# Order of the first loads, the sixth product's second accumulator, and the bank of a values' step in a hybrid encoder layer on one core

## The chip, the core and the metric

The kernel runs on one core of a Trainium2 chip. The metric is the device time of one execution in microseconds. All arithmetic that reaches the output is fp32; a product is formed from operands split in a high and a low part ("hi" and "lo"), with three matmuls (hi x hi, hi x lo, lo x hi) that add up in one accumulator in PSUM.

## What is computed

One encoder layer, for a prompt of 512 tokens and a sample of 1024 tokens, width 1024, with shared weights (cut to what matters):

```python
def _trunk(x, ...):
    h = _rmsnorm(x, norm_attn_g)
    z = h @ w_in
    q, k, v, ca, cb = parts of z
    a_out = _window_attn(q, k, v, bias, band, attn_sink)
    c = _dwconv(ca * sigmoid(cb), conv_dw_w, conv_dw_b)
    c = silu(_layernorm(c, conv_ln_g, conv_ln_b))
    x = x + concatenate([a_out, c]) @ w_out
    h = _rmsnorm(x, norm_ffn_g)
    u = _dwconv(h @ w_up, ffn_dw_w, ffn_dw_b)
    x = x + (silu(u[..., :D_FF]) * u[..., D_FF:]) @ w_down
    return _rmsnorm(x, norm_final_g)
```

## The kernel before

The work is laid out with channels on the 128 partitions and 512 tokens in a row: column tile `nt` = 0 is the prompt, 1 and 2 are the halves of the sample. Each engine runs its own list of instructions in order; the lists are set ahead of the run by a scheduler. From L1340 on TensorE's list follows the program as it is written, and from L1681 on SyncE's too. So a change of a buffer can move rows on an engine, in places where the source is the same. SyncE (SP) issues nearly all transfers; ScalarE (ACT) issues a few.

**The head.** x of the prompt comes transposed in eight pieces of 128 rows (`load_xT(0)`, L200), the weights of the first two projections in five pieces (`load_first`, L221; `PIECES` gives the first row block and the count of each). `first_pieces` scales and splits them: ScalarE makes the hi part of x (L471) and of the weights (L482), GpSimd the lo part of the weights (L483). `beside` (L516) then runs the two projections side by side over the eight row blocks, three matmuls each and block. It does so first for `nt` = 0, then for `nt` = 1, whose x (`load_xT(1)`, tile names `q<-in_laid_xsT`) comes behind the prompt's rows (`load_rows(0)`).

**The projections.** `step(i, nt)` takes a bank of PSUM, runs the 24 matmuls of one projection (`proj`, L305 to L307), and `evac` takes the result out, by its kind: queries, keys, values, or the convolution's two inputs. From about the middle of this phase, `use["step"]` is `"b"`: projections have the two banks b0 and b1 to themselves, while attention (`attention`, L640, L682, L696, and others) runs on the banks a and u between them. A bank is given back when the last Python reference to its tile goes, and the next request takes the first one that is free.

The values' kind ("v") is one of the last branches of `evac`: VectorE multiplies the projection by the row scales (L443) from PSUM into SBUF, a second bank `pt` is taken, four transposes write it (L446), and ScalarE and VectorE read it for the hi and the lo part (L453, L454). `step` holds the projection's bank until `evac` returns.

**The down-projection.** It is done as seven products of half-size matrices (`ORDER` is 1, 2, 5, 6, 7, 4, 3, so the product with `i` = 4 is the sixth). `down_step` runs step `p` of product `i`; there are 11 steps for a product (one step covers 2 x 128 of the 2816 rows, halved by the method). Here TensorE and SyncE follow the written program; the other lists are scheduled. In a step, `mm_down` adds three matmuls (L1514 to L1516) to each of six blocks `tt` of the output. The accumulators are wide tiles of two banks: `pd[0]` holds `tt` 0 and 1, `pd[1]` holds 2 and 3, `pd[2]` holds 4 and 5. There are four wide tiles in all. A product takes `pd[0]` and `pd[1]` at step 0, and `pd[2]` at step `hold` (3 for `i` = 4), where it makes up for the steps that it left out. When a product ends, `evacuate` reads its three accumulators out, by VectorE's adds at L1059 for `i` = 7, and they are free after that. So the sixth product begins with the one free tile for `pd[0]`, and `pd[1]` is the first one that the fifth product (`i` = 7) gives back. `load_x1` fetches a quarter of the residual in six transfers (L1526), and `with_x` adds it to a finished part in three adds, one on VectorE and two on GpSimd.

The lines that set what is edited:

```python
        if p == 0:
            pd.extend(wide() for _ in range(2))
        hold = 5 if i == ORDER[0] else HZ if i == 4 else HOLD
        if p == hold:
            pd.append(wide())
        for tt in range(4):
            mm_down(pd[tt // 2][:, (tt % 2) * NT:(tt % 2 + 1) * NT], i, p, tt)
```

Of the kernel before, what the change touches and what calls it, by code (L numbers as in the profile page):

```python
# [18 lines left out]
NT = 512  # L19
# [40 lines left out]
SA, N2, SA2 = 4, 99, 4  # L60
KL, WN = 16, 7
LN = 3
SUM_AT = (4, 6, 8, 10, 12, 14, 16, 18)
XP, HZ = (1, 3, 3, 6), 3
LZ = 6
# [39 lines left out]
def tile_hybrid_encoder(ctx: ExitStack, tc: tile.TileContext, xs, rel_bias, norm_attn_g, w_in,  # L105
# [19 lines left out]
    def bank(job):  # L125
        return banks.tile([NT], among=use[job])
# [91 lines left out]
    def load_first(i, queue):  # L218
        k0, n = PIECES[i]
        first_w.append(sb.tile([n, 2 * P]))  # L220
        queue.dma_start(first_w[i][:], laid["w_first"][k0:k0 + n].rearrange("k p c -> p k c"))  # L221

    nc.scalar.activation(warm[:], nhalf[:], AF.Exp)
    x_of_prompt = load_xT(0)
    for i in range(2):
        next(x_of_prompt)
        load_first(i, nc.sync)
    for i in range(2, len(PIECES)):
        load_first(i, nc.scalar)
    drawn(x_of_prompt)  # L230
    load_rows(0)
    drawn(load_xT(1))
# [149 lines left out]

    tanh_t, cpads, kt, vt = {}, {}, {}, {}

    def evac(kind, c, nt, src):
        g, n = (0, 0) if nt == 0 else (1, nt - 1)
        rb = rbs[nt]
        T = GR[g]["T"]
        cols = slice(n * NT, (n + 1) * NT)
        if kind == "cb":  # L390
            t = sb.tile([NT])
            nc.vector.tensor_tensor(t[:], src, rb[:], op=ALU.mult)
            nc.scalar.activation(t[:], t[:], AF.Tanh, scale=0.5)
            tanh_t[nt, c] = t
        elif kind == "ca":
            if g == 0:
                cp = sb.tile([T + 64])
                nc.gpsimd.memset(cp[:, 0:PAD], 0.0)
                nc.gpsimd.memset(cp[:, PAD + T:2 * PAD + T], 0.0)
                cpads[g, c] = cp  # L400
            elif n == 0:
                cp = cpads[g, c] = sb.tile([2, PH])
                nc.gpsimd.memset(cp[:, :, 0:LEADIN], 0.0)
                nc.gpsimd.memset(cp[:, :, LEADIN + NT:2 * LEADIN + NT], 0.0)
            cp = cpads[g, c]
            nc.vector.tensor_tensor(src, src, rb[:], op=ALU.mult)
            t = tanh_t.pop((nt, c))[:]
            if g == 0:
                out = cp[:, PAD:PAD + NT]
            else:  # L410
                at = LEADIN + n * NT // 2
                out = cp[:, :, at:at + NT // 2].rearrange("p h k -> p k h")
                t, src = (a.rearrange("p (k h) -> p k h", h=2) for a in (t, src))
            nc.vector.scalar_tensor_tensor(out, t, 1.0, src, op0=ALU.add, op1=ALU.mult)
        elif kind == "q":
            hi, lo = sb.tile([NT], F32R), sb.tile([NT], F32R)
            f = sb.tile([NT])
            nc.vector.scalar_tensor_tensor(f[:], src, QSCALE, rb[:], op0=ALU.mult, op1=ALU.mult)
            nc.scalar.copy(hi[:], f[:])
            nc.gpsimd.tensor_tensor(lo[:], f[:], hi[:].bitcast(F32), op=ALU.subtract)  # L420
            for e in range(2):
                for L, s in ((0, hi), (1, lo)):
                    nc.sync.dma_start(
                        qsd[nt][:, L * HD:(L + 1) * HD, 2 * c + e, :].rearrange("b p t -> p b t"),
                        s[e * HD:(e + 1) * HD, :].bitcast(F32).rearrange("p (b t) -> p b t", t=P))
        elif kind == "k":
            hi, lo = sb.tile([NT], F32R), sb.tile([NT], F32R)
            nc.vector.tensor_tensor(src, src, rb[:], op=ALU.mult)
            nc.scalar.copy(hi[:], src)
            nc.vector.tensor_tensor(lo[:], src, hi[:].bitcast(F32), op=ALU.subtract)  # L430
            for kv in range(NKV):
                if g == 0:
                    kt[0, kv] = [sb.tile([T], F32R) for _ in range(2)]
                for L, s in ((0, hi), (1, lo)):
                    src_k = s[kv * HD:(kv + 1) * HD, :].bitcast(F32)
                    if g == 0:
                        for half in range(2):
                            nc.sync.dma_start(kt[0, kv][L][half * HD:(half + 1) * HD, :].bitcast(F32), src_k)
                    else:
                        nc.sync.dma_start(ksd[:, kv, L, cols], src_k)  # L440
        else:
            vs = sb.tile([NT])
            nc.vector.tensor_tensor(vs[:], src, rb[:], op=ALU.mult)  # L443
            pt = bank("step")
            for i in range(4):
                nc.tensor.transpose(pt[:, i * P:(i + 1) * P], vs[:, i * P:(i + 1) * P], ident[:])  # L446
            src = pt[:].rearrange("p (b c) -> p b c", c=P)
            vs = []
            for kv in range(NKV):
                v = sb.tile([4, P], F32R)  # L450
                head = slice(kv * HD, (kv + 1) * HD)
                rest = slice((1 - kv) * HD, (2 - kv) * HD)
                nc.scalar.copy(v[:, :, head], src[:, :, head])  # L453
                nc.vector.tensor_tensor(v[:, :, rest], src[:, :, head], v[:, :, head].bitcast(F32), op=ALU.subtract)  # L454
                if g == 1:
                    nc.sync.dma_start(vsd[:, n, kv], v[:].bitcast(F32))
                vs.append(v)
            if g == 0:
                vt[0] = vs
# [37 lines left out]

    def step(i, nt):
        kind, c, col = order[i]
        pp = bank("step")  # L500
        proj(pp[:], ws[i], h1[nt])
        landed(i, nt, pp)

    def landed(i, nt, pp):
        kind, c, col = order[i]
        evac(kind, c, nt, pp[:])
        if kind == "ca" and nt != 1:
            g = min(nt, 1)
            (convs, late)[g].append((conv_items, late_items)[g](c, cpads.pop((g, c))))
        tick()  # L510
# [64 lines left out]
    for nt in range(3):  # L575
        if nt:
            pps.update({(nt, c): bank("step") for c in range(2)})
            for kc in range(KC):
                beside(nt, kc)
        if nt == 1:  # L580
            for kc in range(KC):
                raw_h1(2, kc)
            want_w(2)
            row_scale(1)
            want_raw(3)
            load_rows(2)
            constants()
        if nt == 2:
            row_scale(2)
            want_w(3)  # L590
        for i in range(2):
            landed(i, nt, pps.pop((nt, i)))
    for i in range(2):
        ws.pop(i)
    for i in range(2, npr):
# [640 lines left out]
    def wide():  # L1236
        return wide_banks.tile([W2])
# [363 lines left out]
    def make(k):  # L1601
        nonlocal made
        while made <= min(k, len(steps) - 1):
            i, p = steps[made]
            operands(i, p)
            made += 1
# [5 lines left out]
    def down_step(k):  # L1612
        i, p = steps[k]
        if k > 1:
            next(rest, None)
        load_next(8 if k == 0 else 3 if len(pr) < CAP else 0)
        make(k + (LEAD + max(0, min(2, (k - 60) // 2)) if k else 1))
        if p == 0:
            pd.extend(wide() for _ in range(2))
        hold = 5 if i == ORDER[0] else HZ if i == 4 else HOLD  # L1620
        if p == hold:
            pd.append(wide())
        for tt in range(4):
            mm_down(pd[tt // 2][:, (tt % 2) * NT:(tt % 2 + 1) * NT], i, p, tt)
        hl[i, p] = None, hl[i, p][1]
        if p >= hold:
            for q in range(p + 1) if p == hold else (p,):
                for tt in (4, 5):
                    mm_down(pd[2][:, (tt % 2) * NT:(tt % 2 + 1) * NT], i, q, tt)
                hl.pop((i, q)), hp.pop((i, q))  # L1630
        if i == 6 and p == 3:
            load_x1(0, 0)
        if i == 6 and p == 7:
            with_x("o11", 0, 0)
        if i == 7 and p == 4:
            load_x1(0, 1)
        if i == 7 and p == 8:
            with_x("o12", 0, 1)
        if i == 4 and p == XP[0]:
            load_x1(1, 1)  # L1640
            fins.append(sb.tile([D]))
            nc.sync.dma_start(fins[0][:], norm_final_g.partition_broadcast(P))
            nc.scalar.activation(fins[0][:], fins[0][:], AF.Identity, scale=D ** 0.5)
        if i == 4 and p == XP[1]:
            with_x("e", 1, 1)
        if i == 4 and p == XP[2]:
            load_x1(1, 0)
        if i == 4 and p == XP[3]:
            with_x("u", 1, 0)
        if p == NPAIR - 1:  # L1650
            evacuate(i, pd)
            while pd:
                pd.pop(0)
# [156 lines left out]
```

## Time and profile before

| | us |
|---|---|
| median of 3 runs | 1501.6 |
| the runs | 1500.83, 1501.6, 1505.03 |
| the profiled execution | 1504.36 |
| its span in the trace | 1502.6 |

The profiled execution's granted TensorE clock was 0.997 over the span. A line of a timeline has the start and the duration in us, the engine, the line of the program, the operation, output and inputs, and in brackets the idle time of the engine before it, with what ended it. Matmuls of one engine overlap in the trace, so the distance between two starts, and not the duration, is what one costs. In a table by stage, the columns are the stretch, the busy time of each engine in it with the count of instructions, the granted clock, the busy share of the DMA engines, and GB/s.

The product of 128 x 128 by 128 x 512 is the unit of nearly all of TensorE's work: 6736 instructions, 1475.6 us.

### The profile page before, as it was taken

What the parts mean: (1) busy time and instruction counts of PE and PEld (TensorE: products, weight loads), DVE (VectorE), ACT (ScalarE), POOL (GpSimd) and SP (SyncE); (2) the same over time, 40 slices, a digit from 0 to 9 for tenths busy, and PEclk for the clock granted to TensorE, in tenths of its full rate; (3) what the DMA queues carried; (4) which work ended last, traced back from release to release, by engine and by line L of the source; (5) the groups of instructions that cost most, each with busy time, mean ns of one, the idle gap of its engine ahead of it and who ended that gap; (6) DMA issues with size and microseconds to landing.
All of it is one profiled execution on the core that took longest, in us unless ns stands there. A gap on an engine that the chain in (4) does not pass through costs nothing. (4 is left out here: it accounts for less than half of the span.)

```text
span 1502.6 us, 19890 instructions
## 1 busy us (share of the span) xinstructions
PE 1475.6 (98%) x6736; PEld 1213.3 (81%) x6736; DVE 1108.8 (74%) x1512; ACT 802.9 (53%) x1421; POOL 775.7 (52%) x687
## 2 busy tenths in 40 slices
PE   8999999999999999999999999999999999999998
PEld 7888778777888888878888788888888888888786
DVE  7877935648999895575768888888886856567673
ACT  7424455567777876653455444455444553433355
POOL 3454353356977875432436656665654241135656
PEclk9999999999999999999999999999999999999999
DMA  9554241744434454763114433333332494456644
GB/s 377 182 150 146 84 113 36 242 144 133 145 122 134 139 173 130 215 221 112 70 57 140 133 128 128 126 130 123 123 128 90 150 325 157 127 197 205 218 166 156
DMA packets 124625, 228.19 MB, mean 152 GB/s; under 512 B 20419, under 2 KB 45763, under 8 KB 124396
## 3 DMA queue, kind: packets, MB, share of 16 engines
q1 hardware_dynamic: 123276, 225.58, 45.7%
q10 hardware_dynamic: 1248, 1.35, 0.3%
q8 instruction: 53, 0.87, 0.2%
q14 instruction: 48, 0.39, 0.1%
HBM read 166.83 MB, written 61.10 MB: 152 GB/s over the span
## 5 line engine op out<-in xcount | busy, mean ns | idle before, releaser
L159 POOL TENSOR_TENSOR q<-q,q 128x1024 fp32r<-128x1024 f32 x66 | 158.8, 2406 | 84.2 <-ACT q L158 49.7
L1062 POOL TENSOR_TENSOR q<-q,q 128x512 fp32r<-128x512 f32 x81 | 116.6, 1447 | 128.0 <-ACT q L1168 128.0
L1062 DVE TENSOR_TENSOR h<-h,h 128x512 fp32r<-128x512 f32 (+1 forms) x152 | 128.3, 871 | 64.7 <-ACT h L1070 25.6
L1514 PE MATMUL w<-h,h 128*128 128x512 f32 x436 | 170.5, 391 | 2.0 <-DVE q L1059 2.0
L1516 PE MATMUL w<-h,h 128*128 128x512 f32 x436 | 170.1, 390 | 0.0
L1515 PE MATMUL w<-h,h 128*128 128x512 f32 x414 | 161.8, 391 | 0.0
L305 PE MATMUL u<-h,q 128*128 128x512 f32 x384 | 151.1, 394 | 0.0
L307 PE MATMUL u<-h,q 128*128 128x512 f32 x384 | 150.4, 392 | 0.0
L306 PE MATMUL u<-h,q 128*128 128x512 f32 x384 | 150.1, 391 | 0.0
L1182 PE MATMUL w<-h,q 128*128 128x512 f32 x368 | 143.8, 391 | 1.0 <-ACT w L1273 0.6
L1184 PE MATMUL w<-h,q 128*128 128x512 f32 x368 | 143.7, 390 | 0.0
L1183 PE MATMUL w<-h,q 128*128 128x512 f32 x347 | 135.5, 390 | 0.0
L1062 POOL TENSOR_TENSOR h<-h,h 128x512 fp32r<-128x512 f32 (+1 forms) x39 | 54.6, 1401 | 144.1 <-ACT h L1497 113.0
L1070 ACT CAST h<-h 128x512 fp32r<-128x512 f32 x116 | 69.2, 620 | 107.9 <-DVE h L1062 36.8
L158 ACT CAST q<-q 128x1024 fp32r<-128x1024 f32 x66 | 69.3, 1050 | 54.3 <-PE u L306 25.8
L1514 PEld LDWEIGHTS w<-h,h 128*128 128x128 f32 x436 | 82.1, 188 | 19.5 <-DVE q L1059 2.4
L342 DVE SCALAR_TENSOR_TENSOR c<-d,cvw,c 128x512 f32<-128x512 f32 x128 | 95.9, 749 | 1.6
L1516 PEld LDWEIGHTS w<-h,h 128*128 128x128 f32 x436 | 82.3, 189 | 17.2
L1062 POOL TENSOR_TENSOR c<-q,c 128x512 fp32r<-128x512 f32 x46 | 73.1, 1599 | 40.1 <-ACT c L1168 40.0
L1515 PEld LDWEIGHTS w<-h,h 128*128 128x128 f32 x414 | 78.2, 189 | 16.3
L334 POOL TENSOR_TENSOR h<-h,h 128x512 f32<-128x512 f32 x62 | 80.6, 1303 | 14.7 <-ACT h L333 12.5
L307 PEld LDWEIGHTS u<-h,q 128*128 128x128 f32 x384 | 72.1, 188 | 14.8
(459 smaller groups left out, 4005.3 us busy)
## 6 DMA issues: line engine op xcount, KB each, us to landing
q<-in_laid_w_up SPq DMA_DIRECT2D x88, 512.0 KB, 4.0
ga<-q SPq DMA_DIRECT2D x65, 256.0 KB, 2.2
h<-gap SPq DMA_DIRECT2D x57, 256.0 KB, 3.5
h<-ga SPq DMA_DIRECT2D x57, 256.0 KB, 3.6
h<-in_w_down SPq DMA_DIRECT2D x52, 256.0 KB, 3.8
q<-in_laid_w_in SPq DMA_DIRECT2D x22, 512.0 KB, 4.0
gap<-h SPq DMA_DIRECT2D x44, 256.0 KB, 3.1
q<-in_x_sample SPq DMA_DIRECT2D x15, 512.0 KB, 7.2
```

Source lines behind the costliest of these rows:

```text
L159: (nc.vector if dve else nc.gpsimd).tensor_tensor(lo[:], raw[:], hi[:].bitcast(F32), op=ALU.subtract)
L305: nc.tensor.matmul(out, whi[:, kc, :], hi[:], start=(kc == 0), stop=False)
L306: nc.tensor.matmul(out, whi[:, kc, :], lo[:], start=False, stop=False)
L307: nc.tensor.matmul(out, wlo[:, kc, :], hi[:], start=False, stop=(kc == KC - 1))
L342: nc.vector.scalar_tensor_tensor(acc[:], src(t), w(t), acc[:], op0=ALU.mult, op1=ALU.add)
L1062: (eng or nc.vector).tensor_tensor(out, a, b, op=ALU.subtract)
L1182: nc.tensor.matmul(out, whi[:, s], hi[:], start=(start and c == 0), stop=False, **go)
L1183: nc.tensor.matmul(out, whi[:, s], lo[:], start=False, stop=False, **go)
L1184: nc.tensor.matmul(out, wlo[:, s], hi[:], start=False, stop=(stop and c == 3), **go)
L1514: nc.tensor.matmul(out, sh[:, c], th[:], start=(p == 0 and not seeded), stop=False, **go)
L1515: nc.tensor.matmul(out, sh[:, c], tl[:], start=False, stop=False, **go)
L1516: nc.tensor.matmul(out, sl[:, c], th[:], start=False, stop=(p == NPAIR - 1), **go)
```

## The change

Three edits.

```diff
+AHEAD = (1, 1, 1, 2, 2)
+XQ, H2, LATE2 = (1, 5), 2, (4,)
...
     x_of_prompt = load_xT(0)
-    for i in range(2):
-        next(x_of_prompt)
+    next(x_of_prompt)
+    for i, n in enumerate(AHEAD):
         load_first(i, nc.sync)
-    for i in range(2, len(PIECES)):
-        load_first(i, nc.scalar)
+        for _ in range(n):
+            next(x_of_prompt)
     drawn(x_of_prompt)
...
-    def evac(kind, c, nt, src):
+    def evac(kind, c, nt, box):
+        src = box[0][:]
...
             pt = bank("step")
+            box.clear()
             for i in range(4):
...
-        pp = bank("step")
-        proj(pp[:], ws[i], h1[nt])
+        pp = [bank("step")]
+        proj(pp[0][:], ws[i], h1[nt])
         landed(i, nt, pp)
...
-        evac(kind, c, nt, pp[:])
+        evac(kind, c, nt, pp)
...
-            landed(i, nt, pps.pop((nt, i)))
+            landed(i, nt, [pps.pop((nt, i))])
...
+        late = H2 if i in LATE2 else 0
         if p == 0:
-            pd.extend(wide() for _ in range(2))
+            pd.append(wide())
+        if p == late:
+            pd.append(wide())
...
-        for tt in range(4):
-            mm_down(pd[tt // 2][:, (tt % 2) * NT:(tt % 2 + 1) * NT], i, p, tt)
-        hl[i, p] = None, hl[i, p][1]
+        for t0, since in ((0, 0), (2, late)):
+            if p >= since:
+                for q in range(p + 1) if p == since else (p,):
+                    for tt in (t0, t0 + 1):
+                        mm_down(pd[tt // 2][:, (tt % 2) * NT:(tt % 2 + 1) * NT], i, q, tt)
+        if p >= late:
+            for q in range(p + 1) if p == late else (p,):
+                hl[i, q] = None, hl[i, q][1]
...
-        if i == 7 and p == 4:
+        if i == 7 and p == XQ[0]:
             load_x1(0, 1)
-        if i == 7 and p == 8:
+        if i == 7 and p == XQ[1]:
             with_x("o12", 0, 1)
```

**The head.** All five pieces of weights go on SyncE's queue, each behind the piece of x that it is used with. ScalarE's list at its start, before (L482 casts weights, L471 scales x; `h_2`, `h_5`, `h_6`, `h_4`, `h_7` are the weight pieces 0, 2, 3, 1, 4 and `h_1`, `h_3`, `h_8` the first three pieces of x):

```order
L221 DMA h_5_99<-in_laid_w_first 128x2x256
L221 DMA h_6_101<-in_laid_w_first 128x2x256
L221 DMA h_7_103<-in_laid_w_first 128x2x256
L471 ACTIVATE h_24_165<-h_1_91,vecs 128x512
L482 CAST h_22_163<-h_2_93 128x256
L482 CAST h_30_191<-h_5_99 128x512
L471 ACTIVATE h_28_179<-h_3_95,vecs 128x512
L482 CAST h_36_215<-h_6_101 128x512
L482 CAST h_26_177<-h_4_97 128x256
L482 CAST h_42_239<-h_7_103 128x512
L471 ACTIVATE h_32_193<-h_8_105,vecs 128x512
```

And of the change, where the weight pieces are `h_2`, `h_4`, `h_6`, `h_8`, `h_11` in their order:

```order
L475 ACTIVATE h_24_165<-h_1_91,vecs 128x512
L486 CAST h_22_163<-h_2_93 128x256
L475 ACTIVATE h_28_179<-h_3_95,vecs 128x512
L486 CAST h_26_177<-h_4_97 128x256
L475 ACTIVATE h_32_193<-h_5_99,vecs 128x512
L486 CAST h_30_191<-h_6_101 128x512
L475 ACTIVATE h_34_199<-h_7_103,vecs 128x512
L486 CAST h_36_215<-h_8_105 128x512
L475 ACTIVATE h_38_217<-h_9_107,vecs 128x512
L475 ACTIVATE h_40_223<-h_10_109,vecs 128x512
L486 CAST h_42_239<-h_11_111 128x512
```

ScalarE issues none of these transfers any more, and it handles the pieces in the order in which TensorE uses them; GpSimd's five subtractions follow the same order. TensorE's list is unchanged here.

**The values' step.** The projection's bank goes back to the pool ahead of `pt`, so the next projection takes that one. TensorE's list at the first values' step of the sample, before (`b_49` is `pt`, `b_52` the next projection, `a_...` and `u_...` are the attention's):

```order
L446 MATMUL b_49_1502<-ident,h_242_1500 128x128 x4
L682 MATMUL u_56_1583<-ident,h_225_1370 128x128
L682 MATMUL u_56_1583<-ident,h_226_1376 128x128
L682 MATMUL u_56_1583<-ident,h_227_1390 128x128
L682 MATMUL u_56_1583<-ident,h_228_1396 128x128
L640 MATMUL a_60_1655<-h_153_871,h_245_1516 128x384
L640 MATMUL a_60_1655<-h_154_872,h_245_1516 128x384
L682 MATMUL u_55_1567<-ident,h_225_1370 128x128
L682 MATMUL u_55_1567<-ident,h_226_1376 128x128
L682 MATMUL u_55_1567<-ident,h_227_1390 128x128
L682 MATMUL u_55_1567<-ident,h_228_1396 128x128
L305 MATMUL b_52_1532<-h_84_409,q_210_1284 128x512
```

And of the change, the first rows there:

```order
L450 MATMUL b_49_1502<-ident,h_242_1500 128x128 x4
L307 MATMUL b_52_1532<-h_84_409,q_210_1284 128x512
L308 MATMUL b_52_1532<-h_85_410,q_210_1284 128x512
L309 MATMUL b_52_1532<-h_84_409,q_211_1285 128x512
L307 MATMUL b_52_1532<-h_86_413,q_210_1284 128x512
L308 MATMUL b_52_1532<-h_87_414,q_210_1284 128x512
```

The projection's 24 matmuls now stand right behind the transposes. The rows of `u_56` stand between its nineteenth and twentieth matmul, and those of `a_60` and `u_55` behind its last. From here to the end of the sample's attention scores and the prompt's output projection, TensorE's rows change places in 59 pieces of the difference between the two lists, those of the sixth product among them.

**The sixth product.** `pd[1]` is taken at step 2 and makes up for steps 0 and 1 there. The residual for "o12" is loaded at step 1 and added at step 5 of the product with `i` = 7 (steps 4 and 8 before); on SyncE's queue its six transfers stand ahead of five loads of operands that they stood behind. TensorE's list where the second accumulator begins, before (`w_60` is `pd[0]`, `w_61` is `pd[1]`):

```order
L1515 MATMUL w_60_13020<-h_2087_12866,h_2084_12861 128x512
L1516 MATMUL w_60_13020<-h_2086_12865,h_2085_12862 128x512
L1514 MATMUL w_61_13021<-h_2086_12865,h_2084_12861 128x512
L1515 MATMUL w_61_13021<-h_2087_12866,h_2084_12861 128x512
L1516 MATMUL w_61_13021<-h_2086_12865,h_2085_12862 128x512
```

And at the same place of the list in the change:

```order
L1519 MATMUL w_60_13020<-h_2087_12869,h_2084_12864 128x512
L1520 MATMUL w_60_13020<-h_2086_12868,h_2085_12865 128x512
L1518 MATMUL w_60_13020<-h_2095_12905,h_2093_12901 128x512
L1519 MATMUL w_60_13020<-h_2096_12906,h_2093_12901 128x512
L1520 MATMUL w_60_13020<-h_2095_12905,h_2094_12902 128x512
```

`w_60` goes on with steps 1 and 2: `w_61` begins as the nineteenth matmul of the product, where it was the seventh. The list is the same again from step 3 on.

## The prediction

> **What bounds the kernel now.** I read the page first, then the waits of TensorE, then a table by stage, and at last the timelines of the stages that the change touches. The page's first part:
>
> ```profile
> span 1502.6 us, 19890 instructions
> PE 1475.6 (98%) x6736; PEld 1213.3 (81%) x6736; DVE 1108.8 (74%) x1512; ACT 802.9 (53%) x1421; POOL 775.7 (52%) x687
> ```
>
> TensorE is busy for 1475.6 of 1502.6 us, so all its idle time is 27 us. The change removes no matmul; it can win only idle time of TensorE and time at a lower clock. The list of TensorE's waits (engine and line; waited for; total, times, longest) names where they are:
>
> ```profile
> PE w L1514 <- DVE q L1059: 2.0, 1, 2.0
> PE b L305 <- DVE h L454: 1.3, 1, 1.3
> PE a L640 <- DVE s L644: 1.1, 1, 1.1
> ```
>
> The first is in the sixth product, the other two in the values' step; the head's two waits are quoted with the head below. These are the places that the diff edits. By stage (busy of PE, PEld, DVE, ACT, POOL, then the granted clock, the DMA share and GB/s):
>
> ```profile
> 2.50:20.00 17.50, 15.17 (x64) 11.41 (x63) 10.58 (x16) 11.67 (x21) 6.87 (x7) 1.00 1.03 392
> 20.00:60.00 40.00, 40.00 (x178) 32.00 (x179) 38.15 (x57) 26.56 (x46) 14.77 (x14) 1.00 0.67 255
> 150.00:162.00 12.00, 9.43 (x40) 7.33 (x39) 11.28 (x25) 5.52 (x15) 2.01 (x6) 0.86 0.32 116
> 162.00:360.00 198.00, 189.79 (x917) 155.10 (x916) 119.38 (x228) 115.75 (x239) 90.46 (x106) 1.00 0.42 128
> 1400.00:1412.00 12.00, 10.01 (x38) 7.75 (x37) 10.82 (x15) 2.32 (x5) 7.65 (x3) 0.86 0.74 250
> ```
>
> Two stretches, around the values' step and at the start of the sixth product, show a granted clock of 0.86 where the others show 1.00. There something is lost beyond the waits.
>
> **The sixth product.** TensorE, start and duration in us:
>
> ```profile
> 1402.39 0.39 PE L1514 MATMUL w<-h,h 128*128 128x512 f32 x1
> ...
> 1403.53 0.39 PE L1516 MATMUL w<-h,h 128*128 128x512 f32 x1
> 1405.91 0.50 PE L1514 MATMUL w<-h,h 128*128 128x512 f32 x1 [2.00 <-DVE q L1059]
> ...
> 1407.40 0.63 PE L1514 MATMUL w<-h,h 128*128 128x512 f32 x1
> ...
> 1410.81 0.39 PE L1516 MATMUL w<-h,h 128*128 128x512 f32 x1
> ```
>
> Six matmuls from 1402.39 to 1403.53 start 0.228 us apart. Then TensorE stands 2.00 us, because its second accumulator is the room of the product before, which VectorE still has to add up. From 1407.40 to 1410.81 eight matmuls take 3.41 us, 0.427 each: half speed, a loss of 3.41 - 8 x 0.228 = 1.6 us. VectorE at that place:
>
> ```profile
> 1404.04 0.69 DVE L1062 TENSOR_TENSOR q<-q,h 128x512 f32<-128x512 f32 x1
> 1404.64 1.22 DVE L1059 TENSOR_TENSOR q<-w,q 128x1024 f32<-128x1024 f32 x1
> ```
>
> The add that frees the room ends at 1404.64 + 1.22 = 1405.86, behind operand work. In the changed order TensorE has 18 matmuls for the first accumulator (steps 0, 1, 2) before it asks for the second: 1402.39 + 18 x 0.228 = 1406.5. The cover is 0.6 us with VectorE as late as before. Twelve matmuls are moved, none added. The wait of 2.0 us goes, and with it, I say, the half-speed stretch behind it: 3.6 us. Both bounds: 0 if VectorE comes over 2.6 us later than now, 3.6 if it comes no later than 0.6 us. I take 3.6, because VectorE's order ahead of this add is as before. Next in line is the third accumulator, at step 3 as before; the add for it stands one operand row (0.69) and its own 1.2 us behind the first, and TensorE asks for it 30 matmuls, 6.8 us, after the second.
>
> With this goes the earlier load of x1: six DMA issues move on SyncE's queue ahead of five operand loads, which come later by six issues, and two adds of 128x1024 on GpSimd (one more on VectorE) come three steps sooner. GpSimd around them:
>
> ```profile
> 1377.90 5.54 POOL L1059 TENSOR_TENSOR q<-q,c 128x1024 f32<-128x1024 f32 x2 [6.25 <-DMA c<-x1d]
> ...
> 1398.27 3.32 POOL L1062 TENSOR_TENSOR h<-h,h 128x512 fp32r<-128x512 f32 x2 [9.48 <-PE w L1515]
> ```
>
> Those adds took 5.54 us, and GpSimd stood idle 6.25 us before and 9.48 us after. The move costs nothing on that cover; without it the five late loads could cost TensorE what six transfers of 128x512 numbers, 262 KB each, take at the 250 GB/s of the table's last row: 6.3 us. In the other direction it may bring VectorE's operand work forward. I take 0.
>
> **The values' step.** TensorE, then VectorE:
>
> ```profile
> 153.00 0.60 PE L446 MATMUL b<-ident,h 128*128 128x128 f32 x4
> 153.68 0.66 PE L682 MATMUL u<-ident,h 128*128 128x128 f32 x4
> 155.41 0.61 PE L640 MATMUL a<-h,h 128*128 128x384 f32 x2 [1.07 <-DVE s L644]
> 156.10 0.63 PE L682 MATMUL u<-ident,h 128*128 128x128 f32 x4
> 158.07 0.73 PE L305 MATMUL b<-h,q 128*128 128x512 f32 x1 [1.35 <-DVE h L454]
> ...
> 161.56 0.40 PE L307 MATMUL b<-h,q 128*128 128x512 f32 x1
> ```
>
> ```profile
> 151.74 0.69 DVE L443 TENSOR_TENSOR h<-b,h 128x512 f32<-128x512 f32 x1 [0.61 <-PE u L697]
> ...
> 157.52 0.40 DVE L454 TENSOR_TENSOR h<-b,h 128x256 fp32r<-128x256 f32 x1
> ```
>
> Before, the next projection takes the bank of the transposes, read until 157.52 + 0.40 = 157.92; hence its start at 158.07. After, it takes the bank that L443 had read by 151.74 + 0.69 = 152.43. The changed order puts its matmuls right behind the transposes of 153.00, and the attention's rows (the L640 that waited 1.07 for VectorE among them) behind or between them. They are delayed by up to 24 x 0.228 = 5.5 us, which is longer than the 1.07 that they lacked. So both waits go, 2.4 us, and so does the half-speed stretch: from 158.07 to 161.56 eight starts take 3.49 where 1.82 would do, 1.7. Together 4.1. The least is 1.35 - 1.07 = 0.3, if the moved attention rows find an equal wait elsewhere and the clock stays; the most is 4.1, since there is no more idle time in the stage to win. I take 4.1, but 0.3 less for the second values' step, where the attention rows that stood between now stand elsewhere: 3.8.
>
> The order of attention and projections changes in many pieces after this place, up to about 330 us. The table above has 198.0 - 189.8 = 8.2 us of idle TensorE between 162 and 360; these waits may shrink or grow. I have no row for a direction, take 0, and keep 3 us each way, about a third of them.
>
> **The head.** TensorE and, last, ScalarE:
>
> ```profile
> 8.25 0.50 PE L516 MATMUL u<-h,h 128*128 128x512 f32 x1 [1.34 <-ACT h L482]
> 10.00 0.50 PE L516 MATMUL u<-h,h 128*128 128x512 f32 x1 [0.56 <-POOL h L483]
> 18.60 0.39 PE L516 MATMUL b<-h,h 128*128 128x512 f32 x1
> 19.03 1.74 PE L516 MATMUL a<-h,h 128*128 128x512 f32 x5
> ```
>
> ```profile
> 18.26 1.34 ACT L471 ACTIVATE h<-q,vecs 128x512 fp32r<-128x512 f32 x2 [1.37 <-DMA q<-in_laid_xsT]
> ```
>
> The casts come in the order of arrival, so w1 was cast behind w2 and w3. In the new order both waits, 1.9 us, go from the first pair of projections. But the next pair, which starts at 19.03, waits for a transfer that lets ScalarE go at 18.26, and the first row of the table shows why: the DMA engines are full (1.03, 392 GB/s) and the bytes ahead of that transfer are the same. The gain becomes idle time of about 2 to 2.5 us before 19.03, since the 40 us after it are solid for TensorE and the load still sets their start. Gain: 0, at best 0.3 from a queue that starts smoother. At worst the new idle time draws a half-speed stretch, 1.7, as it did at both places above (2.00 us in one; 1.07 and 1.35 in the other). I take 0.
>
> This is where a rule bears on the sum. The Trainium skill, "TensorE: Matmul & The Clock Gate", section "What's actually happening", says that the clock falls to half after at least one idle window of about 3.4 us, in windows that run freely. Here it fell after idle time of 2.0 us and of 2.4 us in two pieces, and stayed low for 3.4 us; the length agrees, the threshold does not. By that rule alone the waits would not be what lowers the clock, and removing them would win no clock.
>
> **The sum.** The profiled execution took 1504.36 us (span 1502.6). 1504.36 - 3.6 - 3.8 + 0 = 1497.0. It lies 2.8 above the median of the runs, 1501.6. If a run's clock falls only when a wait lies badly against the clock's own period, some runs have fewer than the two stretches of 3.3 us; with none, waits alone count: 1501.6 - 2.0 - 2.4 = 1497.2. Both ways agree. I predict 1496.8, between them and a small gain from the reordered waits.
>
> **The rivals.**
>
> Rival one, **the waits go, the clock does not follow** (or the head pays it anew): only 2.0 + 2.4 are won, 1504.36 - 4.4 = 1500.0, or 1498.5 with one stretch kept. For it: the head's new gap is as long as the two that had a low clock. Against: in both places the low clock began within 1.5 us of the end of a long wait, and nowhere else in the five stages tabled.
>
> Rival two, **the change doesn't do what it says in the sixth product**: VectorE is later, the wait comes at the second accumulator anyway, and 3.4 to 3.6 are not won: 1500.5. For it: a cover of only 0.6 us. Against: 18 matmuls are 4.1 us, and GpSimd's earlier adds relieve VectorE if they do anything.
>
> Rival three, **the reordering closes more waits**: 3 of the 8.2 us between 162 and 360 go too: 1494. For it: projections now fill places where attention waited. Against: nothing aims at them.
>
> Rival four, **slower: the attention comes late to the end of its phase**. Each of two values' steps lets 24 matmuls pass, 5.5 us, ahead of the softmax's rows. The end of the phase waits already:
>
> ```profile
> 332.00:344.00 12.00, 9.12 (x48) 6.11 (x48) 10.51 (x22) 10.41 (x24) 10.01 (x10) 1.00 0.30 84
> 344.00:360.00 16.00, 13.81 (x65) 11.11 (x64) 13.92 (x24) 13.33 (x25) 8.89 (x6) 1.00 0.48 169
> ```
>
> That is 2.9 and 2.2 us of idle TensorE with VectorE at 10.51 of 12. If both delays came through, 11 us, the time would be 1496.8 + 11 = 1508. It decides from a delay of 9.3 us on (1506.1). Against: over 162 to 360 VectorE is busy for 119.38 of 198 us, so it has 78 us in which to catch up.
>
> **How the numbers follow.** A measurement tells about 0.3% from no change, 4.5 us: faster is below 1497.1, slower above 1506.1. The forecast, 1494.5 to 1499.3, has 0.55: 0.38 of it faster, 0.17 same, as its middle lies at the bound. Rivals one and two together 0.20, all same. Rival three 0.14, all faster. Rival four 0.11: 0.09 slower, 0.02 same. So faster 0.52, same 0.39, slower 0.09. The range takes in rivals one, two and half of three: 1493.0 to 1501.5.
>
> **What would show it.** In the changed trace: no wait of TensorE for the add of L1059 at the start of the sixth product, and clock 1.00 there; the next projection right behind the transposes of the values' step, at about 153.4 instead of 158.07; the first pair of projections done near 16.7, but the second pair starting at 19.0 as now; idle time from 332 to 360 near 5 us. The prediction is wrong if the second pair starts earlier than 18.5, if the low clock shows up without long waits, or if the waits between 162 and 360 change by over 3 us.

## The result, and the profile after

The change makes the kernel slower: 1513.76 us (median of 4 runs, 1509.59 to 1515.01) against 1501.21 us for the kernel before (4 runs, 1500.49 to 1505.03) on the same chip. The ratio is 1.0077, with a 95% interval from 1.0063 to 1.0091. The profiled execution of the changed kernel is its shortest, 1509.59 us; in it the mean granted clock was 0.995, in the three others 0.990 to 0.992. Over 1510 us each thousandth of the clock is 1.5 us, so the clock alone is enough for the 3.4 to 5.4 us between these runs. Among the runs further down, three executions of 2479, 3008 and 8477 us are slow ones, and the ratios leave them out.

The page of the changed kernel begins:

```profile
span 1507.8 us, 19891 instructions
PE 1478.7 (98%) x6736; PEld 1215.6 (81%) x6736; DVE 1113.5 (74%) x1512; ACT 803.2 (53%) x1421; POOL 778.0 (52%) x687
```

The list of TensorE's waits (what waits; for what; total, times, longest) has other names at its top than before:

```profile
PE a L700 <- ACT h L688: 4.3, 4, 2.4
PE u L790 <- DVE q L795: 2.6, 1, 2.6
PE a L520 <- ACT h L475: 2.6, 1, 2.6
PE a L701 <- DVE q L689: 1.3, 1, 1.3
```

The add behind the fifth product (L1059 before, L1063 now) and the values' subtraction (L454, now L458) are gone from it. The next projection stands right behind the transposes of the values' step:

```profile
154.97 0.60 PE L450 MATMUL b<-ident,h 128*128 128x128 f32 x4
155.33 0.47 PE L307 MATMUL b<-h,q 128*128 128x512 f32 x1
```

The same stages as before, with one more around 290 us (busy of PE, PEld, DVE, ACT, POOL, granted clock, DMA share, GB/s), for the changed kernel:

```profile
20.00:60.00 40.00, 39.95 (x174) 32.63 (x173) 36.88 (x55) 25.37 (x45) 13.97 (x13) 0.96 0.65 252
150.00:162.00 12.00, 12.00 (x62) 10.22 (x61) 11.30 (x24) 5.30 (x14) 2.04 (x5) 1.00 0.44 152
275.00:305.00 30.00, 23.18 (x86) 17.46 (x85) 18.60 (x27) 13.99 (x28) 9.40 (x11) 0.83 0.80 267
1400.00:1412.00 12.00, 12.00 (x55) 9.92 (x54) 9.21 (x14) 3.98 (x7) 3.58 (x4) 1.00 0.66 194
```

And the new one for the kernel before:

```profile
275.00:305.00 30.00, 28.94 (x133) 23.65 (x132) 19.41 (x31) 14.01 (x27) 10.24 (x15) 1.00 0.95 298
```

Both places that the prediction priced are won: 150 to 162 and 1400 to 1412 are full, at clock 1.00. But between 275 and 305 us TensorE's idle time grew from 30 - 28.94 = 1.1 to 30 - 23.18 = 6.8 us, and the clock fell to 0.83, which is another 30 x 0.17 = 5.1 us. In the head the clock is 0.96 over 40 us, 1.6 us. The account of the two profiled executions: -4.2 (values' step), -3.7 (sixth product), +5.7 and +5.1 (275 to 305), +0.5 and +1.6 (head) is +5.0; the spans differ by 5.2. That is less than the 12.6 us between the medians, because the profiled execution of the kernel before lies 3.2 us above its median and that of the changed kernel 4.2 below.

What happened at 276 us is seen in TensorE's timelines. Before:

```profile
276.99 0.60 PE L745 MATMUL u<-ident,h 128*128 128x128 f32 x4
277.34 0.48 PE L305 MATMUL b<-h,q 128*128 128x512 f32 x1
...
279.74 0.39 PE L306 MATMUL b<-h,q 128*128 128x512 f32 x1
279.97 0.39 PE L696 MATMUL a<-h,h 128*128 128x512 f32 x1
```

After:

```profile
276.20 0.40 PE L309 MATMUL b<-h,q 128*128 128x512 f32 x1
276.43 0.60 PE L764 MATMUL a<-ident,h 128*128 128x128 f32 x4
276.87 0.60 PE L749 MATMUL u<-ident,h 128*128 128x128 f32 x4
...
278.72 0.40 PE L792 MATMUL u<-h,h 128*128 128x512 f32 x1
281.56 0.49 PE L700 MATMUL a<-h,h 128*128 128x512 f32 x1 [2.44 <-ACT h L688]
283.35 0.79 PE L701 MATMUL a<-q,h 128*128 128x512 f32 x1 [1.30 <-DVE q L689]
...
300.33 0.80 PE L790 MATMUL u<-h,h 128*128 128x512 f32 x1 [2.62 <-DVE q L795]
```

L745 and L760 (now L749 and L764) are transposes of the convolution's norm; L696 (now L700) is the attention's product, with the high part of its operand from ScalarE (L684, now L688) and the low part from VectorE (L685, now L689). Before, eleven matmuls of the last projection (`b`, L305 to L307) stand ahead of the product, 2.5 us of work. After, the last projection is over at 276.20. Six matmuls of the output projection (L790 to L792) follow, and then nothing stands between them and the product: L700 comes at 281.56, 1.6 us later than its counterpart before.

The operands are late as well. ScalarE, before:

```profile
275.35 0.60 ACT L684 CAST h<-a 128x512 fp32r<-128x512 f32 x1
...
279.84 1.25 ACT L818 CAST h<-h 128x512 fp32r<-128x512 f32 x2 [2.33 <-DMA h<-in_laid_w_out]
```

After:

```profile
276.29 1.14 ACT L822 CAST h<-q 128x512 fp32r<-128x512 f32 x2 [0.63 <-DMA q<-in_laid_w_out]
...
279.00 0.62 ACT L822 CAST h<-h 128x512 fp32r<-128x512 f32 x1 [0.54 <-DMA h<-in_laid_w_out]
279.53 1.50 ACT L770 ACTIVATE q<-a,vecs 128x128 f32<-128x128 f32 x4
280.91 0.59 ACT L688 CAST h<-a 128x512 fp32r<-128x512 f32 x1
```

Before, the product's cast ends at 275.95 and VectorE's low part at 276.80, more than three microseconds ahead of the product, so the product did not need the eleven matmuls as cover. After, the cast stands in ScalarE's list behind seven casts of the output projection's weights (L822, from 273.67 on), for whose transfers ScalarE stands idle 3.4 us, and behind L770; it ends at 281.50. Before, two of these casts stood ahead of it. The traces of `r1_values`, `r2_val_nt2` and `r2_val_rows` below have the seven, that of `r2_val_nt1` the two.

The third wait has another path. VectorE's rows of the changed kernel:

```profile
289.00 1.52 DVE L774 TENSOR_TENSOR h<-q,h 128x512 fp32r<-128x512 f32 x1
...
299.58 1.29 DVE L795 TENSOR_TENSOR q<-u,q 128x512 f32<-128x512 f32 x2 [4.75 <-DMA q<-in_x_prompt]
```

and the issue of x of the prompt's first block on SyncE's queue, after and before:

```profile
290.55 0.33 SPq L149 DMA_DIRECT2D q<-in_x_prompt  x1
```

```profile
284.31 1.67 SPq L147 DMA_DIRECT2D q<-in_x_prompt  x3
```

That block of x goes into the buffer whose last reader is L774, a step of the convolution's norm; it ends at 290.52. But SyncE's list comes to this request only at 290.42, so the buffer holds it for 0.1 us; in the trace of `r1_values` below the step (L772 there) ends at 287.46, and the request is issued at 290.52 all the same. What makes it late is its place in SyncE's list, last of the four blocks and behind a transfer of keys (`ksd`) and two of `bbd`. Before, the last three blocks were issued together from 284.31 on. The rows don't name the blocks; that the late one is the block that the add needs is tested below by another order of x. The add that frees the bank of the output projection waits for it until 299.58, nine microseconds behind the issue; the DMA share of the stage is 0.80.

### The profile page after: what moved, and what is told of

The parts are those of the page before. It is cut to its first block, busy times and chain, and to the rows that moved or that the text cites. A ratio compares the mean times of both kernels' runs of the same rounds, so it can differ in the third digit from the quotient of the medians.

```text
span 1507.8 us, 19891 instructions
## 1 busy us (share of the span) xinstructions
PE 1478.7 (98%) x6736; PEld 1215.6 (81%) x6736; DVE 1113.5 (74%) x1512; ACT 803.2 (53%) x1421; POOL 778.0 (52%) x687
## 4 chain that ended last, share of the span: by engine, by line
PE 83%; DVE 5%; DMA 4%; POOL 3%; ACT 2%; issue 2%; SPq 0%; POOLq 0%; DVEq 0%; ACTq 0%
PE w L1186 8%; PE w L1187 8%; PE w L1188 8%; PE w L1519 7%; PE w L1518 7%; PE w L1520 7%; PE u L307 6%; PE u L308 6%; PE u L309 6%; PE b L307 2%; PE b L309 2%; PE b L308 2%; PE a L644 1%; PE a L686 1%; PE u L790 1%
## 5 line engine op out<-in xcount | busy, mean ns | idle before, releaser
L1520 PE MATMUL w<-h,h 128*128 128x512 f32 x432 | 168.1, 389 | 0.0
L1518 PE MATMUL w<-h,h 128*128 128x512 f32 x432 | 168.1, 389 | 0.0
L1519 PE MATMUL w<-h,h 128*128 128x512 f32 x412 | 160.3, 389 | 0.0
L307 PE MATMUL u<-h,q 128*128 128x512 f32 x384 | 151.0, 394 | 0.0
L1518 PEld LDWEIGHTS w<-h,h 128*128 128x128 f32 x432 | 81.1, 188 | 16.9
L1520 PEld LDWEIGHTS w<-h,h 128*128 128x128 f32 x432 | 81.1, 188 | 16.9
L1519 PEld LDWEIGHTS w<-h,h 128*128 128x128 f32 x412 | 77.3, 188 | 16.0
```

Source lines behind the costliest of these rows:

```text
L307: nc.tensor.matmul(out, whi[:, kc, :], hi[:], start=(kc == 0), stop=False)
L1518: nc.tensor.matmul(out, sh[:, c], th[:], start=(p == 0 and not seeded), stop=False, **go)
L1519: nc.tensor.matmul(out, sh[:, c], tl[:], start=False, stop=False, **go)
L1520: nc.tensor.matmul(out, sl[:, c], th[:], start=False, stop=(p == NPAIR - 1), **go)
```

## The experiments

Each is timed in rounds with the kernel before on the same chip; the kernel before has 29 runs for each group of four. The three edits turned out to be independent in the order of the engines: the head's moves no row of TensorE or VectorE, the sixth product's none before 1300 us. The values' edit stands at three steps, one for the prompt and one for each half of the sample; the engines' rows are in the same order as before up to 153 us, so the prompt's step moved nothing.

**The values' edit alone.**

```diff
-    def evac(kind, c, nt, src):
+    def evac(kind, c, nt, box):
+        src = box[0][:]
...
             pt = bank("step")
+            box.clear()
```

> Only the values' edit. Theory A (this edit alone makes the loss at 275 to 305 us, by the order of the attention and the projections that it sets): 4.1 us less at 150 to 162, as in the changed kernel, and at 275 to 305 waits of 6 to 7 us instead of 1.1, with two or more half-speed stretches of 3.4 us; time 1506 to 1513. Theory B (the loss needs the head's edit too, which delays everything by half a microsecond and lets transfers collide): no more than 2 us of waits at 275 to 305, time 1496 to 1498.

1513.43 us against 1500.71, ratio 1.0086 (1.0068 to 1.0104). No wait at 153 to 158, and all of the loss, 0.4 us above the range that was expected. The list of its waits between 275 and 305 us:

```profile
PE u L788 <- DVE q L793: 6.6, 1, 6.6
PE a L698 <- ACT h L686: 2.4, 1, 2.4
PE a L699 <- DVE q L687: 1.1, 1, 1.1
```

With two small ones the waits there are 10.8 us, where 6 to 7 were expected. Theory A holds and B falls: neither the head nor the sixth product is needed for the loss.

**The sixth product's edits alone** (the diff as above, without the other two parts).

> Only the sixth product's edits. Theory A: the wait of 2.0 us at its start goes, and in the runs where it drew a half-speed stretch that goes too; everything up to 1350 us as before; time 2.0 to 3.7 below the kernel before, 1497.5 to 1499.2. Theory B says the same of this one.

1498.88 against 1500.71, ratio 0.9991 (0.9979 to 1.0003). The wait is gone from the trace. By the medians it is 1.8 us, just under the 2.0 to 3.7 that were expected; the interval reaches from 3.1 us less to 0.5 more, and cannot by itself be told from no change.

**The head's edit alone.**

```diff
+    next(x_of_prompt)
+    for i, n in enumerate(AHEAD):
         load_first(i, nc.sync)
+        for _ in range(n):
+            next(x_of_prompt)
```

> Only the head's edit. Theory A: the second pair of projections starts about 0.5 us later (19.6), TensorE idle 2.6 us before it, a half-speed stretch behind in part of the runs; everything later as before but moved; time 0.5 to 2.2 above the kernel before, 1501.7 to 1503.4. Theory B: with this edit the transfers around 275 to 300 collide otherwise, and waits there grow from 1.1 to several us: 1505 or more.

1501.89 against 1500.71, ratio 1.0004 (0.9993 to 1.0016): no gain and no loss that can be told. The trace shows the gap, and behind it matmuls at half speed (a pair of them takes 1.16 to 1.20 us instead of 0.7):

```profile
18.40 0.39 PE L517 MATMUL b<-h,h 128*128 128x512 f32 x1
20.51 2.98 PE L517 MATMUL a<-h,h 128*128 128x512 f32 x8 [1.72 <-ACT h L472]
...
23.57 1.20 PE L517 MATMUL a<-h,h 128*128 128x512 f32 x2
```

**The head's edit with its gap filled.**

```diff
     first_w.clear()
+    fill = bank("conv")
+    for i in range(11):
+        nc.tensor.matmul(fill[:], ws[i % 2][0][:, KC - 1, :], h1[0][KC - 1][0][:], start=True, stop=True)
+    fill = None
```

> The head's edit, and 11 matmuls of 128x512 whose results nobody reads, into the free bank c behind and among the last ones of the first pair, so that TensorE works through the gap. If idle time is what lowers the clock, the half-speed stretch behind the gap is gone in every run although the second pair starts no earlier: time 0.5 above the kernel before, about 1501.7, up to 1.7 less than the head's edit alone. If the clock falls there for another reason (the clock's own period, the transfers), the stretch is at 20 us again and the two times agree.

1501.41, ratio 0.9999 (0.9987 to 1.0010). In its trace TensorE has no gap there and no half-speed stretch:

```profile
19.50 1.52 PE L527 MATMUL c<-h,h 128*128 128x512 f32 x6
20.86 1.98 PE L517 MATMUL a<-h,h 128*128 128x512 f32 x8
...
23.39 0.70 PE L517 MATMUL a<-h,h 128*128 128x512 f32 x2
```

Eight matmuls take 1.98 us here and 2.98 there. One profile of each agrees with idle time as the cause of the low clock. The times differ by 0.5 us, less than their intervals, and don't decide it.

**The values' edit for one half of the sample at a time.**

```diff
             pt = bank("step")
+            if nt == 1:
+                box.clear()
```

and the same with `nt == 2`.

> The values' edit for the sample's first half alone (nt = 1). Theory C (the loss belongs to the second values' step, nt = 2, behind which the projections get so far ahead of the attention that none are left to cover it at 276 us): the two waits at 153 to 158 are gone, at 275 to 305 waits of 1 to 2 us as before the change; 2.4 to 4.1 below the kernel before, 1496.6 to 1498.5. Theory D (any projection that runs ahead at 153 is paid back at 276): waits of 4 us or more at 275 to 305, 1501 or more.

> The values' edit for the sample's second half alone (nt = 2). Theory C: the waits of 1.1 and 1.35 us at 153 to 158 as before the change, and at 275 to 305 the whole loss, 6 to 10 us of waits and two or more half-speed stretches; 1508 to 1517. Theory D: half of the loss, 1504 to 1507.

For `nt` = 1: 1499.90 against 1501.74, ratio 0.9987 (0.9977 to 0.9996). For `nt` = 2: 1517.25, ratio 1.0102 (1.0079 to 1.0125). The loss belongs to the second step alone, as theory C said, and is 15.5 us, at the upper end of what it said: waits of 4.0 us between 275 and 305, and the add's 4.6 us just behind, at 306. The two steps' -1.8 and +15.5 add up to 13.7, near the 12.7 of the whole edit. In the traces, 772 of the 864 matmuls of projections (L305 to L307 before) stand ahead of the norm's transposes L760 at 253.64 us in the kernel before and at the same place with `nt` = 1, and 795 with `nt` = 2 and in the change; ahead of the transposes L745 at 276.99, 852 in the first two, and all 864 in the others.

But the first step wins 1.8 us where 2.4 to 4.1 were expected. Theory D has a part in it. TensorE's waits between 305 and 360 us, with `nt` = 1:

```profile
PE a L643 <- DVE h L709: 2.7, 1, 2.7
PE u L305 <- DVE h L954: 2.0, 1, 2.0
PE c L264 <- DVE q L847: 1.5, 1, 1.5
PE a L685 <- ACT h L958: 0.8, 1, 0.8
```

and in the kernel before:

```profile
PE a L696 <- ACT h L684: 1.7, 2, 1.4
PE c L264 <- DVE q L844: 1.3, 1, 1.3
PE a L640 <- DVE h L706: 0.8, 1, 0.8
PE a L682 <- DVE s L644: 0.8, 1, 0.8
```

That is 7.0 us against 4.6: of the 4.2 won at 153 by the profiled executions, 2.4 are waited for again at the end of the phase.

**The values' edit, with x asked for in another order.** The first block gets a buffer that is free earlier in the schedule; only the buffers' names change, and which block has which place in SyncE's list.

```diff
-    for i in range(4):
+    for i in (2, 1, 0, 3):
         xr[i] = load_x(*blocks[i])
```

> The values' edit, and the prompt's four blocks of x for the output projection asked for in the order 2, 1, 0, 3, so that the first block that is needed no longer gets the buffer that VectorE reads last (L774 of the late convolution norm). Theory E (the long wait at 294 to 300 is that row of x, issued late for its buffer): the wait for the DVE add at 294 falls from 6.6 us to under 1.5, the waits at 276 to 285 stay; 3 to 8 us below the values' edit alone, 1505 to 1510. Rival: the row is late because the transfers are dense there, whichever buffer it has; then 1512 or more.

1505.07 against 1501.74, ratio 1.0023 (1.0011 to 1.0036); the values' edit alone had 1.0086. The difference of the ratios is 0.0063, 9.5 us, though from two chips' runs of the kernel before. The wait for the add is gone between 275 and 305 us, and the first two remain:

```profile
PE a L698 <- ACT h L686: 2.9, 1, 2.9
PE a L699 <- DVE q L687: 0.6, 1, 0.6
PE a L762 <- DVE h L756: 0.3, 1, 0.3
```

Theory E holds in that the wait was for this row. SyncE issues the four blocks from 269.1 to 289.4 us, much as before, with another one in the last place; that the buffer's reader holds the row back is not what the traces show. The gain is more than the wait of 6.6 us: in the two profiled executions, time at half speed up to 1490 us falls as well, from 23.9 to 10.2 us.

**The kernel before with that order of x**, the control.

> The kernel before with only the order 2, 1, 0, 3 in which the prompt's blocks of x are asked for: the control for the row order. Theory E (the row order wins what it wins because the values' edit makes that row late): here the wait of 1.1 us at 292 goes or halves, time 0 to 1.1 below the kernel before, at most 1.7 more if a half-speed stretch went with it. Rival (the row order is worth 8 us by itself): 1494 or less.

1500.66 against 1502.71, ratio 0.9988 (0.9976 to 1.0000). The wait of 1.1 us at 292 is gone from its trace. The gain by the medians is 2.1 us, more than the 1.1 expected, and the interval reaches from 3.6 less to none. So most of the 9.5 us is won from the late row that the values' edit makes, and not from the row order as such.

**The two halves of the sixth product's edit.** Only the accumulator (`H2`, with `load_x1` and `with_x` at steps 4 and 8), and only the residual (steps 1 and 5, with both accumulators at step 0).

> Of the sixth product's edits only the second accumulator at step 2, with the residual's loads and adds where they were. Theory A: the wait of 2.0 us goes, as TensorE has 18 matmuls before it needs the room: 2.0 less, 1499 to 1500. Rival (the earlier residual is needed too, since VectorE is late behind GpSimd): a wait of 1 us or more stays at the second accumulator, and the time is within 1 us of the kernel before.

> Of the sixth product's edits only the residual of the first block loaded at step 1 and added at step 5 of the product before. Theory A: the wait at the start of the sixth product stays between 1.4 and 2.0 us, time within 0.5 us of the kernel before. Rival: GpSimd's earlier adds let VectorE reach its add sooner, and the wait falls under 1 us by this edit alone.

The accumulator alone: 1499.81 against 1502.71, ratio 0.9980 (0.9971 to 0.9989). The residual alone: 1500.75, ratio 0.9984 (0.9975 to 0.9993). Each removes the wait entirely, and here I was wrong about the second one. VectorE's rows with the residual alone:

```profile
1400.51 0.69 DVE L1062 TENSOR_TENSOR q<-q,h 128x512 f32<-128x512 f32 x1 [0.27 <-DMA q<-in_w_down]
1401.12 1.22 DVE L1059 TENSOR_TENSOR q<-w,q 128x1024 f32<-128x1024 f32 x1
```

The add starts at 1401.12 instead of 1404.64, 3.5 us earlier; 1.0 of it comes from the execution, since with the old residual the add starts at 1403.68 in the trace of `r3_rows`. Earlier transfers and adds bring VectorE's operand work forward by some 2.5 us. The two halves are covers for one wait, and do not add up.

**The parts that won, together**: the values' edit for `nt` = 1, the sixth product's edits, without and with the row order.

> The values' edit for nt = 1 alone, and the sixth product's edits. Theory C: both gains add up, no wait at 153 to 158 nor at 1404; 4.4 below the kernel before by the waits, 7 with the half-speed stretches that they drew: 1493.5 to 1497. Theory D: 1498 or more.

> The values' edit for nt = 1 alone, the sixth product's edits, and the row order 2, 1, 0, 3: the parts that won by themselves. If they add up: 2.7 below the kernel before from the first two as measured, and up to 1 us from the row order, 1497 to 1499. If the wait before 330 us, which grew from 0.8 to 2.7 with the values' edit, takes up what comes earlier: no better than without the row order.

Without: 1499.00 against 1501.74, ratio 0.9980 (0.9971 to 0.9990). Theory C had 1493.5 to 1497, and the time is in theory D's range: the parts win 1.8 and 1.8 us by themselves, and 2.7 together. With: 1497.93 against 1502.71, ratio 0.9962 (0.9948 to 0.9976), 5 runs from 1495.87 to 1498.24, within 1497 to 1499 as expected; the intervals of the two ratios overlap, so a gain from the row order here is not shown. This one beats both the kernel before and the changed one. The wait near 329 us is 2.5 us in it, as with `nt` = 1 alone; that part of the gain stays lost.

## Why the prediction was wrong

It said 1496.8 us, and faster or the same with 0.91; the kernel is slower by 12.6. The step that failed is the zero for the order of attention and projections up to 330 us, in the third point.

- **What bounds the kernel.** Right in general: only idle time and half-speed time of TensorE changed. But the argument treated TensorE's time as one sum, from which a removed wait is subtracted to the end. In the phase up to 360 us that is not so: the runs fit a chain through the attention and the convolution's norm on ScalarE and VectorE that decides when the phase is over, with projections as its cover. With `nt` = 1, 2.4 of 4.2 us come back as waits there.
- **The sixth product, 3.6.** The mechanism was right: no wait, clock 1.00. The size against the median is smaller: 1.8 less by the whole edit (3.1 less to 0.5 more), 2.9 and 2.0 less by its halves. The profiled execution that gave 3.6 was an unlucky one: eight traces have this wait, 1.0 to 2.0 us long, and only that one has a half-speed stretch behind it. "I take 0" for the earlier residual was wrong; by itself it removes the wait. Nor is "VectorE's order ahead of this add" as before: with the sixth product's edits it changes from 1322 us on.
- **The values' step, 3.8.** Local reading right: the projection stands right behind the transposes (155.33 behind 154.97), both waits and the low clock are gone. The step that failed is the next sentence: "I have no row for a direction, take 0, and keep 3 us each way" for the order up to 330 us. The runs put 12.7 us on the values' edit, and all of it on its second step (15.5 by itself), which the prediction had charged with 0.3. In place of zero, the projections that ran ahead were used up at 276 us, the product's cast was late in ScalarE's list, and a block of x late in SyncE's.
- **The direction could have been read.** The order of the change shows the last projection used up ahead of the transposes L745, where the trace of before has eleven matmuls of it behind them. The prediction counted the pieces that moved, and did not go through them for the last one.
- **Rival four** had the right sign and, in general, the right cause, attention falling behind projections. Its place was wrong (332 to 360, and it came at 276), and it had 0.11, because VectorE's 78 us of idle time were taken as room to catch up. That room lies elsewhere: from 280 to 285 us of the changed kernel VectorE is busy for 5.00 of 5.00 us. That its price of 11 us for both steps is near the 12.7 measured is luck: it had no part in it for the row of x, nor for the half-speed stretches, and the first step does not lose but win.
- **The head, 0.** Right within what was stated: 1.2 more, from 1.0 less to 2.4 more. "The second pair starting at 19.0 as now" was not: the second pair starts at 19.57 in the profiled execution, and the 2.60 us of idle time before it is followed by a half-speed stretch.
- **The clock.** Rival one held that the clock may not follow the waits. In the changed kernel half speed came behind the new waits of 2.60, 2.44 and 2.62 us. But that full speed came where waits went shows little, since most executions have full speed there with the waits: eight traces keep the waits of 1.1 and 1.3 us at the first values' step, and five of them have no stretch behind. So the 3.3 us of clock in the prediction's two terms belonged to one execution. The Trainium skill, "TensorE: Matmul & The Clock Gate", section "What's actually happening", says that the window runs freely, so that the place of a change depends on where in it the work lies. The traces agree in that: in each with two stretches or more, these begin a whole number of 3.413-us periods apart, 366 before (158.11 and 1407.39 us), 77 and 5 in the changed kernel (20.16, 282.99 and 300.05). The section's idle time of a whole window, about 3.4 us, before the clock falls is not what these runs show: 1.72 us was followed by half speed.

One link is not isolated by a run of its own: that the first two waits at 276 to 285 us come with the order that the second step's edit sets is shown by the two halves of the values' edit, but how much of them is the missing cover and how much the late cast on ScalarE is not. An estimate from the timelines: the eleven matmuls, 2.5 us, would have covered the first wait of 2.44, and operands as early as before would have left neither wait. A kernel that gives the attention its old place behind the second values' step with the bank given back early was not tried.

## What to carry to other kernels

Work that an engine can do at any time is the cover of a chain that it must wait for; a change that lets it run ahead spends the cover early, and the wait comes back where the cover is used up. So with a change that only lets a scheduler move rows, follow the moved rows on every engine to the last piece of the flexible work, look what stands behind it, what now stands ahead of its operands on the other engines, and which transfers the new lists ask for later. And try each place of an edit by itself: the same line won 1.8 us at one step and lost 15.5 at the next.

## What the runs showed of the hardware

Idle time of TensorE of 1.7 to 2.6 us was followed by stretches of half speed of 3.41 us or twice that: in the changed kernel most matmuls from 283.94 to 288.92 us take 0.63 us each instead of 0.39. In these traces, whether a wait draws one goes with where it falls on the grid of 3.413-us periods. In the three traces with a stretch behind the first values' step, one period has 1.6 to 2.1 us of idle time, from parts of both waits; in the five without, no period there has more than 1.4 us. Elsewhere the bound is less sharp: a period with 1.8 us of idle time was once not followed by a stretch (`r3_nt1_sixth_rows`, 747 us).

Runs of one kernel differ in part by this: the kernel before had 29 runs from 1497.72 to 1505.54 us on one chip, with mean clocks from 0.994 to 1.000, but one with 1.000 took 1501.31 and one with 0.996 took 1499.58. A gain of 2 us therefore took 10 runs and more on each side to see, and a single profiled execution can carry 3 us of it in places where most have less.
